# Weight sums in DRAM for every group of seven products, four groups more, and a new place for the sums of the second slot

## The chip, the cores and the metric

The kernel runs on one core of one Trainium2 chip. The metric is the device time of one execution in microseconds (us). Three runs of the kernel before gave a median of 2503.86 us, from 2502.97 to 2507.02.

The engines have short names in the profile: PE is the matrix engine (PEld its weight loads), DVE the vector engine, ACT the scalar engine, POOL the general-purpose engine and SP the engine that issues most DMAs. Each works through its own instructions in program order and waits on semaphores for the others.

## What is computed

256 tokens of width 2048 in fp32 go through two layers. Cut to what matters here:

```python
# layer 0: Mamba-2 mixer, then SwiGLU
h = h + mamba2_mixer(rmsnorm(h, a_norm_w), a_in_proj, ...)   # y = ssd(...) * silu(z); grouped rmsnorm; y @ out_proj
h = h + swiglu(rmsnorm(h, ffn_norm_w[0]), w_gate_up[0], w_down[0])
# shared keys, values and forget gates; layer 1: attention, then SwiGLU
k, v, cum = shared_kv(h, ...)
h = h + forgetting_attention(rmsnorm(h, b_norm_w), k, v, cum, w_q, q_norm_w, w_o)
h = h + swiglu(rmsnorm(h, ffn_norm_w[1]), w_gate_up[1], w_down[1])

def swiglu(h, w_gate_up, w_down):
    g, u = jnp.split(h @ w_gate_up, 2, axis=-1)
    return (jax.nn.silu(g) * u) @ w_down
```

`out_proj` is 4096 x 2048, `w_o` 2048 x 2048, `w_gate_up` 2048 x 11264 and `w_down` 5632 x 2048. Nearly all of the time is the products with these weights and with `in_proj`, `w_kvf` and `w_q`.

## The kernel before

**Weights.** All weights stream once from DRAM. The unit of a load is 512 KB, a tile `wraw` of 128 partitions by 1024 floats (two rows of 128 contracted values by 512 columns). There are six such buffers (`RAW`), and SP issues the next load when a buffer comes free. Each product is made in three matmuls of a shorter float type: ACT casts the unit to `whi` (`split_hi`, L271), DVE subtracts that from the unit to give `wlo` (`split_lo`, L277), and PE multiplies activation hi by weight hi, hi by lo and lo by hi (L563 to L565). A piece is one such split, used by six matmuls for a group, or twelve for an ordinary unit. Four pieces can be split ahead (`SPL`), so the cast of one piece waits until PE has finished the piece four before it. ACT, DVE and PE thus form a line with four places between its ends.

**Activations.** Each block of 512 activation channels lies transposed in a *slot* (tile `xT`, its hi and lo part). A projection's contracted width is cut into such slots, numbered kg.

**Groups of seven.** `pair` takes two neighbouring column blocks of an output. For most kg it makes their eight products in the plain way. For the kg in the tuple `crossed` it uses a scheme of Winograd's, seven products of six matmuls (L475, L476, L478) in place of eight. It needs sums of weights and sums of activations. The activation sums (tile `xS`) are made per slot in `sums_from` (four DVE operations, L624 to L627, then a cast by ACT and a subtraction by DVE), after an addition in `add_sums` (L641). `out_stage` makes those of some slots with the slot (`summed`) and others after the whole stage (`later`). The weight sums come in two ways:

- In the gate-and-up projections (`made=True`, pieces in the order f d c a e g b) a group loads five units. Two of them, c and a, are sums that were made in DRAM, and DVE makes two more additions (L429).
- In the out and down projections (`made=False`, order d g a c e b f) a group loads four units, and DVE makes four additions (L429).

The out projection of layer 0 (here *out0*) has groups at kg 4 and 6 of 8 (`WOUT`), the down projection of layer 0 (*dn0*) at 3 and 7, that of layer 1 (*dn1*) at 3, 6 and 9 of 11 and the attention's output projection (*wo*) at 2, each for two pairs of column blocks. The gate-and-up projections (*ffn0*, *ffn1*) have 20 groups each.

**Sums in DRAM.** `next_sum` takes one step: SP copies one weight unit to a DRAM tile `wsum` (L376), and POOL adds the partner of the sum begun before to it with an accumulating DMA (L378), once that copy has landed. The stream of loads calls it at every sixth load up to load 224 and at every twelfth after (`PACE`). Should a group's sum not be made when its load comes up, `load` calls `next_sum` until it is (L392). The load then follows on SP, where it waits until the accumulation has landed, and every later load stands behind it.

**Order.** The program is one stream of pieces. Everything else (normalisation, gates, the transposes into slots) is written as tasks in three queues (`urgent`, `mid`, `lazy`), which a planner works off between pieces. There is one exception: at piece d of a pair's first group `cross_step` (L452) empties the first two queues (`flow.finish_all(False)`, L463), whatever is in them, before it goes on.

**The gates before out0.** `z_done(g)` makes the gate of slot g of the eight that out0 contracts, and `gate_y` (L1064) finishes that slot: two products on DVE (L1069), two sums of squares on ACT (L1072), a root on DVE and POOL (L580, L582), two scalings on ACT (L1077), then transposes on PE (L595), cast by ACT (L273) and subtracted by DVE (L279). The slots 6 and 7 are finished while out0 is already running. After the last gate, `add_sums` is called for the slots in `WOUT`.

Of the kernel before, what the change touches and what calls it, by code (L numbers as in the profile page):

```python
# [230 lines left out]
def kernel(ctx: ExitStack, tc: tile.TileContext, xT_d, x_d, cols_d, rows_d, wdt_d, win_d,  # L231
# [191 lines left out]
    def split_cross(group, name):  # L423
# [7 lines left out]
        if group.cross.made:  # L431
            place, dead = {"e": "c", "b": "c"}, {"f": "f", "c": "d", "a": "a", "g": "g", "b": "c"}
            early, late = {}, {"c": ("c", "c", "d"), "e": ("c", "c", "g")}
        else:
# [6 lines left out]
        split_hi(hi, src)  # L441
        if name in early:
            add(*early[name])
        split_lo(hi, lo, src)
# [945 lines left out]
```

## Time and profile before

| | us |
|---|---|
| median of three runs | 2503.86 |
| lowest and highest of them | 2502.97, 2507.02 |
| the profiled execution | 2506.06 |
| its span in the trace | 2504.3 |
| PE busy in the span | 2482.6 |
| DVE busy | 1997.2 |
| ACT busy | 1425.8 |
| POOL busy | 105.4 |

The profiled execution is 2.2 us above the median. The span is what the profiler recorded; the other 1.8 us lie around it. A row of a time line reads: start, duration, engine, line of the kernel, operation, output and inputs; behind it, in brackets, how long the engine had been idle and what released it.

### The profile page before, as it was taken

The numbers are of one execution on the slowest core, as the hardware profiler recorded it, in microseconds if no ns is written. First come the engines' busy times: TensorE is split into PE (matmuls) and PEld (weight loads), VectorE is DVE, ScalarE is ACT, GpSimd is POOL, SyncE is SP. The second block draws the span as 40 slices with busy tenths as digits, with TensorE's granted clock in tenths as the row PEclk, the third lists the DMA queues.
The fourth block names the chain that finished last, engine by engine and source line by source line (L and its number), as shares of the span: only waits on it lengthen the run. The fifth ranks groups of instructions, "written<-read, shape, count | busy, mean of one in ns | idle before, by whom it ended". The sixth has DMA issues, their size and how long they took to land.

```text
span 2504.3 us, 31677 instructions
## 1 busy us (share of the span) xinstructions
PE 2482.6 (99%) x11434; PEld 2056.0 (82%) x11434; DVE 1997.2 (80%) x2569; ACT 1425.8 (57%) x1791; POOL 105.4 (4%) x132
## 2 busy tenths in 40 slices
PE   9999999999999999999999999999999999999999
PEld 7888888887878888888888888888878888888887
DVE  6677777778688999997767657678789898988867
ACT  6665566555456656564445556565565656555544
POOL 0000000000000000000000011010000000000000
PEclk9999999999999999999999999999999999999999
DMA  9887868677777888788676777665668776765564
GB/s 302 274 250 232 254 209 259 217 231 248 236 247 239 273 264 268 253 271 253 211 245 209 238 216 232 190 193 179 231 218 273 257 257 214 241 203 194 206 232 142
DMA packets 160205, 586.13 MB, mean 234 GB/s; under 512 B 17808, under 2 KB 18464, under 8 KB 158512
## 3 DMA queue, kind: packets, MB, share of 16 engines
q1 hardware_dynamic: 147024, 531.59, 61.8%
q0 software_dynamic: 13024, 52.52, 11.1%
q8 instruction: 90, 1.47, 0.2%
q14 instruction: 67, 0.55, 0.1%
HBM read 581.85 MB, written 86.07 MB: 267 GB/s over the span
## 4 chain that ended last, share of the span: by engine, by line
PE 93%; DVE 3%; DMA 2%; ACT 1%; issue 1%; SPq 0%; ACTq 0%; DVEq 0%
PE acc L564 23%; PE acc L563 23%; PE acc L565 23%; PE mis L476 4%; PE mis L478 4%; PE mis L475 4%; PE acc L475 3%; PE acc L476 3%; PE acc L478 3%; DVE wlo L277 2%; PE mis L595 1%; PE mis L1032 1%; DVE wraw L429 1%; DMA wraw<-in_wout_dram 1%; ACT whi L271 1%
## 5 line engine op out<-in xcount | busy, mean ns | idle before, releaser
L271 ACT CAST whi<-wraw 128x1024 fp32r<-128x1024 f32 (+1 forms) x956 | 982.9, 1049 | 699.6 <-PE acc L565 466.0
L277 DVE TENSOR_TENSOR wlo<-wraw,whi 128x1024 fp32r<-128x1024 f32 (+1 forms) x953 | 1140.4, 1220 | 299.8 <-ACT whi L271 291.3
L563 PE MATMUL acc<-whi,xT 128*128 128x512 f32 x2528 | 994.9, 394 | 5.4 <-ACT whi L271 4.1
L564 PE MATMUL acc<-wlo,xT 128*128 128x512 f32 x2528 | 986.2, 390 | 3.1 <-DVE wlo L277 3.1
L565 PE MATMUL acc<-whi,xT 128*128 128x512 f32 x2528 | 986.0, 390 | 0.0
L563 PEld LDWEIGHTS acc<-whi,xT 128*128 128x128 f32 x2528 | 475.4, 188 | 104.8 <-ACT whi L271 5.7
L564 PEld LDWEIGHTS acc<-wlo,xT 128*128 128x128 f32 x2528 | 475.7, 188 | 102.1 <-DVE wlo L277 5.8
L565 PEld LDWEIGHTS acc<-whi,xT 128*128 128x128 f32 x2528 | 475.3, 188 | 99.8
L279 DVE SCALAR_TENSOR_TENSOR wlo<-wraw,cols,whi 128x512 fp32r<-128x512 f32 x192 | 134.7, 747 | 72.1 <-ACT whi L273 71.7
L429 DVE TENSOR_TENSOR wraw<-wraw,wraw 128x1024 f32<-128x1024 f32 x144 | 176.4, 1225 | 6.2 <-DMA wraw<-in_wout_dram 1.4
L273 ACT ACTIVATE whi<-wraw,cols 128x512 fp32r<-128x512 f32 x192 | 127.6, 717 | 72.1 <-PE acc L565 55.1
L476 PE MATMUL mis<-wlo,xS 128*128 128x512 f32 x336 | 131.4, 391 | 2.8 <-DVE wlo L277 2.8
L475 PE MATMUL mis<-whi,xS 128*128 128x512 f32 x336 | 130.9, 390 | 0.7 <-DVE xT L277 0.7
L478 PE MATMUL mis<-whi,xS 128*128 128x512 f32 x336 | 130.7, 389 | 0.0
L378 POOL DMA_DIRECT2D wsum<-in_gu_dram x80 | 66.5, 831 | 1406.2 <-DMA wsum<-in_gu_dram 1379.1
L476 PE MATMUL acc<-wlo,xT 128*128 128x512 f32 x216 | 84.4, 391 | 2.1 <-DVE wlo L277 2.1
L475 PE MATMUL acc<-whi,xT 128*128 128x512 f32 x216 | 84.1, 389 | 0.0
L478 PE MATMUL acc<-whi,xT 128*128 128x512 f32 x216 | 84.1, 389 | 0.0
L476 PEld LDWEIGHTS mis<-wlo,xS 128*128 128x128 f32 x336 | 63.1, 188 | 18.1 <-DVE wlo L277 5.1
L475 PEld LDWEIGHTS mis<-whi,xS 128*128 128x128 f32 x336 | 63.0, 188 | 14.2 <-DVE xT L277 1.1
L478 PEld LDWEIGHTS mis<-whi,xS 128*128 128x128 f32 x336 | 63.1, 188 | 12.9
L271 ACT CAST xT<-mis 128x512 fp32r<-128x512 f32 x52 | 27.9, 589 | 52.4 <-PE mis L595 52.4
(241 smaller groups left out, 2050.3 us busy)
## 6 DMA issues: line engine op xcount, KB each, us to landing
wraw<-in_gu_dram SPq DMA_DIRECT2D x312, 512.0 KB, 5.6
wraw<-in_dn_dram SPq DMA_DIRECT2D x176, 512.0 KB, 5.5
wraw<-in_win_dram SPq DMA_DIRECT2D x159, 512.0 KB, 6.1
wsum<-in_gu_dram SPq DMA_DIRECT2D x80, 512.0 KB, 6.6
wsum<-in_gu_dram POOLq DMA_DIRECT2D x80, 512.0 KB, 8.3
wraw<-wsum SPq DMA_DIRECT2D x80, 512.0 KB, 4.7
wraw<-in_wout_dram SPq DMA_DIRECT2D x64, 512.0 KB, 6.4
wraw<-in_wq_dram SPq DMA_DIRECT2D x32, 512.0 KB, 4.5
```

What stands on the lines that cost most here:

```text
L271: nc.scalar.copy(out=hi, in_=src)
L273: nc.scalar.activation(hi, src, AF.Copy, scale=scal)
L277: nc.vector.tensor_tensor(out=lo, in0=src, in1=hi.bitcast(F32), op=ALU.subtract)
L279: nc.vector.scalar_tensor_tensor(out=lo, in0=src, scalar=scal, in1=hi.bitcast(F32), op0=ALU.mult, op1=ALU.subtract)
L378: nc.gpsimd.dma_start(out=old.tile, in_=old.other, accum_op=ALU.add)
L429: nc.vector.tensor_tensor(out=us[out].raw, in0=us[in0].raw, in1=us[in1].raw, op=ALU.add)
L475: nc.tensor.matmul(ps, lhsT=xh, rhs=hi[:, p, :], start=group.first and p == 0 and name not in own, stop=False)
L476: nc.tensor.matmul(ps, lhsT=xh, rhs=lo[:, p, :], start=False, stop=False)
L478: nc.tensor.matmul(ps, lhsT=xl, rhs=hi[:, p, :], start=False, stop=stop and p == 1)
L563: nc.tensor.matmul(b.ps[t], lhsT=xh, rhs=hi[:, j, :], start=u is b.units[0] and ks[j] == 0, stop=False)
L564: nc.tensor.matmul(b.ps[t], lhsT=xh, rhs=lo[:, j, :], start=False, stop=False)
L565: nc.tensor.matmul(b.ps[t], lhsT=xl, rhs=hi[:, j, :], start=False, stop=last and j == len(ks) - 1)
```

## The change

All groups now take the form that only the gate-and-up projections had: five loads, two sums from DRAM, two additions on DVE. Out0 gets groups at kg 2, 4 and 6, and dn1 at 3, 5, 7 and 9, which is one more for each of the two pairs of column blocks, four more in all. There are now 120 sums in DRAM, where there were 80. None is begun in the first 24 loads; from there to load 224 there is one for each six loads, and after that one for each ten. The activation sums of slot 1 of the two gate-and-up projections are made when that slot is made, not after the stage. The sums for out0's slots 2 and 4 are asked for at gate 6, those of slot 6 at gate 7 as before. `add_sums` works in another buffer.

```diff
-WOUT, DN0, DN1 = (4, 6), (3, 7), (3, 6, 9)
+WOUT, DN0, DN1 = (2, 4, 6), (3, 7), (3, 5, 7, 9)
-PACE = (224, 6, 12)
+PACE = (24, 224, 6, 10)
@@ class Cross
-        self.order = "fdcaegb" if made else "dgacebf"
+    ORDER = "fdcaegb"
@@ def pair
+        adjacent = len(crossed) > 1 and crossed[-1] == crossed[-2] + 1
             if kg in crossed:
-                if not (made and kg > crossed[0]):
+                if not (adjacent and kg == crossed[-1]):
                     order += rights
                     rights = []
                 (b11, b21), (b12, b22) = us
-                if made:
-                    c, a = Sum(b22.src, b12.src), Sum(b22.src, b21.src)
-                    sums.extend((c, a))
-                    first = {"f": b12, "d": b21, "c": Unit(None, kg, c, NB, [1, 3]),
-                             "a": Unit(None, kg, a, NB, [1, 3]), "g": b11}
-                else:
-                    first = {"d": b21, "g": b11, "+": b22, "f": b12}
+                c, a = Sum(b22.src, b12.src), Sum(b22.src, b21.src)
+                sums.extend((c, a))
+                first = {"f": b12, "d": b21, "c": Unit(None, kg, c, NB, [1, 3]),
+                         "a": Unit(None, kg, a, NB, [1, 3]), "g": b11}
@@ def split_cross
-            place, dead = {"a": "d", "c": "+", "e": "d", "b": "+"}, {"c": "g", "e": "d", "b": "+", "f": "f"}
-            early = {"g": ("+", "f", "+"), "c": ("d", "f", "d")}
-            late = {"d": ("d", "d", "+"), "c": ("+", "g", "d")}
+        place, dead = {"e": "c", "b": "c"}, {"f": "f", "c": "d", "a": "a", "g": "g", "b": "c"}
+        late = {"c": ("c", "c", "d"), "e": ("c", "c", "g")}
@@ def stream
-                pace = PACE[1] if i < PACE[0] else PACE[2]
-                if i % pace == pace - 1:
+                pace = PACE[2] if i < PACE[1] else PACE[3]
+                if i >= PACE[0] and i % pace == pace - 1:
                     next_sum()
@@ def out_stage
-                for kg in later:
-                    add_sums(nxt[kg])
@@ def ffn_up, took
-                if xs[1].adder is not None:
-                    flow.finish(xs[1].adder)
@@ def z_done
-            if g == G - 1:
+            if g >= G - 2:
                 for kg in WOUT:
-                    add_sums(ys[kg])
+                    if (kg < G - 2) == (g == G - 2):
+                        add_sums(ys[kg])
@@
-    xs2, r2 = out_stage(ys, wout_d, C_F0, WOUT, summed=(2,), later=(1,))
+    xs2, r2 = out_stage(ys, wout_d, C_F0, WOUT, summed=(1, 2))
-    xs4, r4 = out_stage(oT, wo_d, C_F1, (2,), summed=(2,), later=(1,))
+    xs4, r4 = out_stage(oT, wo_d, C_F1, (2,), summed=(1, 2))
```

PE has 10760 instructions in place of 10784, which is 24 matmuls of 512 columns fewer. SP has 60 rows more (20 loads and 40 copies), POOL 40 more (accumulations), and DVE 24 additions fewer. The line numbers of the changed kernel are some 4 to 9 lower than those of the kernel before. Its instructions stand in another order at three places.

**Out0's first pair of column blocks, PE.** In the kernel before, the transposes of slot 7 (inputs `xs`, outputs `mis`) stand between pieces of ordinary units (outputs `acc`), as those of slot 6 do some way ahead of them:

```order
L565 MATMUL acc_4718<-whi_4682,xT_3301 128x512
L563 MATMUL acc_4719<-whi_4682,xT_3301 128x512
L564 MATMUL acc_4719<-wlo_4683,xT_3301 128x512
L565 MATMUL acc_4719<-whi_4682,xT_3301 128x512
L595 MATMUL mis_4778<-ident,xs_2541 128x128 x4
L595 MATMUL mis_4787<-ident,xs_2541 128x128 x4
L563 MATMUL acc_4718<-whi_4712,xT_3301 128x512
L564 MATMUL acc_4718<-wlo_4713,xT_3301 128x512
L565 MATMUL acc_4718<-whi_4712,xT_3301 128x512
```

In the changed kernel the group at kg 2 stands here. After its piece f (the six products with `xS`) come the transposes of slot 6 and then those of slot 7, and piece d only behind both:

```order
L466 MATMUL acc_4601<-whi_4615,xS_4406 128x512
L467 MATMUL acc_4601<-wlo_4616,xS_4406 128x512
L469 MATMUL acc_4601<-whi_4615,xS_4406 128x512
L466 MATMUL acc_4601<-whi_4615,xS_4406 128x512
L467 MATMUL acc_4601<-wlo_4616,xS_4406 128x512
L469 MATMUL acc_4601<-whi_4615,xS_4406 128x512
L586 MATMUL mis_4698<-ident,xs_2529 128x128 x4
L586 MATMUL mis_4707<-ident,xs_2529 128x128 x4
L586 MATMUL mis_4728<-ident,xs_2529 128x128 x4
L586 MATMUL mis_4737<-ident,xs_2529 128x128 x4
L466 MATMUL mis_4746<-whi_4633,xT_3521 128x512
L467 MATMUL mis_4746<-wlo_4634,xT_3521 128x512
```

The queues that piece d empties now hold the ends of two gates, and no product stands between the transposes of the two.

**The same place, ACT.** Before, casts of weights (`whi<-wraw`) stand between the steps of slot 7's gate, from slot 6's transposes in the first row to slot 7's own in the last two:

```order
L273 ACTIVATE xT_4641<-mis_4651,cols 128x256 x2
L1072 ACTIVATE zs_4563,ssg_4660<-xs_2541 128x512
L271 CAST whi_4664<-wraw_4488 128x1024
L271 CAST whi_4682<-wraw_4531 128x1024
L1072 ACTIVATE zs_4565,ssg_4660<-xs_2541 128x512
L271 CAST whi_4712<-wraw_4549 128x1024
L1077 ACTIVATE xs_2541<-xs_2541,rs_4703 128x512 x2
L271 CAST xS_4597<-xsum_4707 128x4x128
L271 CAST whi_4736<-wraw_4581 128x1024
L271 CAST whi_4759<-wraw_4609 128x1024
L273 ACTIVATE xT_4777<-mis_4778,cols 128x256 x2
L273 ACTIVATE xT_4777<-mis_4787,cols 128x256 x2
```

Now, the last cast ahead of the gates' ends is that of piece e, and the next one comes behind both:

```order
L272 CAST whi_4690<-wraw_4509 128x1024
L1069 ACTIVATE xs_2529<-xs_2529,rs_4652 128x512 x2
L274 ACTIVATE xT_4697<-mis_4698,cols 128x256 x2
L274 ACTIVATE xT_4697<-mis_4707,cols 128x256 x2
L1064 ACTIVATE zs_4597,ssg_4716<-xs_2529 128x512
L1064 ACTIVATE zs_4599,ssg_4716<-xs_2529 128x512
L1069 ACTIVATE xs_2529<-xs_2529,rs_4723 128x512 x2
L274 ACTIVATE xT_4727<-mis_4728,cols 128x256 x2
L274 ACTIVATE xT_4727<-mis_4737,cols 128x256 x2
L272 CAST xS_4654<-ysum_4753 128x4x128
L272 CAST whi_4761<-wraw_4552 128x1024
```

The steps of slot 7's gate (its squares and its scaling) moved in between the transposes of slots 6 and 7.

**The start of ffn0, DVE.** Before, the sums of slot 1 (L641, and 624 to 627 with the `xS` subtraction) stand among the splits and additions of the first group:

```order
L277 TENSOR_TENSOR wlo_6145<-wraw_5980,whi_6144 128x1024
L277 TENSOR_TENSOR wlo_6155<-wraw_5956,whi_6154 128x1024
L429 TENSOR_TENSOR wraw_5956<-wraw_5956,wraw_6000 128x1024
L277 TENSOR_TENSOR wlo_6167<-wraw_6000,whi_6166 128x1024
L277 TENSOR_TENSOR wlo_6178<-wraw_5956,whi_6177 128x1024
L624 TENSOR_TENSOR xsum_6195<-y_6123 128x128
L625 TENSOR_TENSOR xsum_6195<-y_6123 128x128
L626 TENSOR_TENSOR xsum_6195<-y_6123,xsum_6195 128x128
L627 TENSOR_TENSOR xsum_6195<-y_6123,xsum_6195 128x128
L277 TENSOR_TENSOR wlo_6201<-wraw_6035,whi_6200 128x1024
L277 TENSOR_TENSOR xS_6194<-xsum_6195,xS_6194 128x4x128
L641 TENSOR_TENSOR y_6215<-xT_5282 128x512
```

Now only splits and additions stand there (L278 is `split_lo`, L428 the addition):

```order
L278 TENSOR_TENSOR wlo_6166<-wraw_6001,whi_6165 128x1024
L428 TENSOR_TENSOR wraw_6001<-wraw_6001,wraw_5966 128x1024
L278 TENSOR_TENSOR wlo_6185<-wraw_6025,whi_6184 128x1024
L278 TENSOR_TENSOR wlo_6195<-wraw_6001,whi_6194 128x1024
L428 TENSOR_TENSOR wraw_6001<-wraw_6001,wraw_6045 128x1024
L278 TENSOR_TENSOR wlo_6207<-wraw_6045,whi_6206 128x1024
L278 TENSOR_TENSOR wlo_6218<-wraw_6001,whi_6217 128x1024
L278 TENSOR_TENSOR wlo_6238<-wraw_6080,whi_6237 128x1024
```

The sums of slot 1 have moved some 80 rows up, into the second pair of out0.

**A late group of ffn1, SP.** Before, the group's two sums are loaded from tiles `wsum` that were copied some hundreds of loads earlier:

```order
L398 DMA wraw_17485<-in_gu_dram 128x1024
L398 DMA wraw_17487<-wsum_12494 128x1024
L398 DMA wraw_17489<-wsum_12858 128x1024
L398 DMA wraw_17502<-in_gu_dram 128x1024
L398 DMA wraw_17515<-in_gu_dram 128x1024
```

Now the copies (L375) stand right among the group's loads, that of the second sum (`wsum_18267`) with one load between it and its own:

```order
L397 DMA wraw_18264<-in_gu_dram 128x1024
L375 DMA wsum_18267<-in_gu_dram 128x1024
L397 DMA wraw_18266<-wsum_18095 128x1024
L375 DMA wsum_18272<-in_gu_dram 128x1024
L397 DMA wraw_18271<-wsum_18267 128x1024
L397 DMA wraw_18287<-in_gu_dram 128x1024
```

From the 81st sum on the copies have caught up with the loads: 13 of the last 40 sums have six or fewer loads between their copy and their own load. Ten of them are in ffn1, with distances of 4, 5, 6, 2, 3, 6, 1, 1, 6 and 1 in their order, and three in dn1, with 1 each. In the kernel before the smallest such distance is 97 loads.

## Rows read from the trace of the kernel before

**Rows 1.** The page, first part: busy us, share of the span, instructions

```profile
span 2504.3 us, 31677 instructions
PE 2482.6 (99%) x11434; PEld 2056.0 (82%) x11434; DVE 1997.2 (80%) x2569; ACT 1425.8 (57%) x1791; POOL 105.4 (4%) x132
```

**Rows 2.** Time line of PE, first and last of 60 matmuls without a pause

```profile
690.72 0.39 PE L563 MATMUL acc<-whi,xT 128*128 128x512 f32 x1
...
704.09 0.39 PE L565 MATMUL acc<-whi,xT 128*128 128x512 f32 x1
```

**Rows 3.** Busy time by stretches: stretch, length, each engine, PEclk, DMA share, GB/s

```profile
560.00:620.00 60.00, 56.23 (x248) 44.69 (x247) 52.38 (x57) 30.31 (x34) 2.52 (x4) 1.00 0.76 233
...
725.00:750.00 25.00, 22.31 (x88) 16.98 (x87) 23.04 (x33) 13.51 (x16) 1.91 (x2) 0.93 0.68 204
...
1205.00:1212.00 7.00, 6.61 (x30) 5.12 (x29) 6.91 (x7) 4.62 (x6) 0.00 (x0) 1.00 0.32 90
1740.00:1760.00 20.00, 18.21 (x85) 14.54 (x84) 18.79 (x26) 10.96 (x18) 0.82 (x1) 1.00 0.95 315
1825.00:1866.00 41.00, 37.16 (x162) 28.96 (x161) 36.62 (x45) 23.43 (x26) 0.81 (x1) 1.00 0.74 231
```

**Rows 4.** Time line at the start of ffn0, PE and ACT

```profile
738.74 0.62 ACT L271 CAST xS<-xsum 128x512 fp32r<-128x512 f32 x1 [2.77 <-DVE xsum L627]
...
740.36 0.50 PE L563 MATMUL acc<-whi,xT 128*128 128x512 f32 x1 [1.05 <-ACT whi L271]
741.62 0.50 PE L564 MATMUL acc<-wlo,xT 128*128 128x512 f32 x1 [0.76 <-DVE wlo L277]
...
742.97 0.63 PE L563 MATMUL acc<-whi,xT 128*128 128x512 f32 x1
```

**Rows 5.** Stretches around a pause at the start of ffn0 and of ffn1

```profile
732.00:746.00 14.00, 11.31 (x40) 7.93 (x39) 12.87 (x20) 7.74 (x10) 0.00 (x0) 0.88 0.71 228
1829.00:1845.00 16.00, 13.26 (x55) 9.72 (x54) 14.87 (x23) 8.57 (x10) 0.00 (x0) 1.00 0.72 240
```

**Rows 6.** Time line in out0: slot 6's transposes, then gate 7's steps

```profile
540.10 1.03 PE L595 MATMUL mis<-ident,xs 128*128 128x128 f32 x8
...
543.90 0.63 ACT L1072 ACTIVATE zs<-xs 128x512 f32<-128x512 f32 x1 [1.60 <-DVE xs L1069]
...
548.12 1.08 POOL L582 TENSOR_TENSOR rs<-ms,mhalf 128x2 f32<-128x2 f32 x1 [12.10 <-DVE ms L580]
...
549.23 1.34 ACT L1077 ACTIVATE xs<-xs,rs 128x512 f32<-128x512 f32 x2 [1.16 <-POOL rs L582]
```

**Rows 7.** The page, DMA issues: count, KB each, median us to landing

```profile
wsum<-in_gu_dram SPq DMA_DIRECT2D x80, 512.0 KB, 6.6
wsum<-in_gu_dram POOLq DMA_DIRECT2D x80, 512.0 KB, 8.3
wraw<-wsum SPq DMA_DIRECT2D x80, 512.0 KB, 4.7
```

**Rows 8.** DMA issues from 1225 to 1250 us, few loads in flight

```profile
wsum<-in_gu_dram SPq DMA_DIRECT2D x1, 512.0 KB, 5.2
wsum<-in_gu_dram POOLq DMA_DIRECT2D x1, 512.0 KB, 5.7
```

**Rows 9.** DMA issues from 1953 to 1962 us, many loads in flight

```profile
wsum<-in_gu_dram SPq DMA_DIRECT2D x1, 512.0 KB, 6.7
wsum<-in_gu_dram POOLq DMA_DIRECT2D x1, 512.0 KB, 9.8
```

**Rows 10.** Time line in ffn1, a second group: load of d, splits of a

```profile
1905.55 0.33 SPq L398 DMA_DIRECT2D wraw<-in_gu_dram  x1
...
1917.65 1.05 ACT L271 CAST whi<-wraw 128x1024 fp32r<-128x1024 f32 x1 [1.67 <-PE acc L565]
...
1918.74 1.23 DVE L277 TENSOR_TENSOR wlo<-wraw,whi 128x1024 fp32r<-128x1024 f32 x1 [0.23 <-ACT whi L271]
...
1921.76 0.39 PE L476 MATMUL mis<-wlo,xS 128*128 128x512 f32 x1
```

**Rows 11.** Time line in ffn1, a first group: load of d, split of a

```profile
1886.96 0.33 SPq L398 DMA_DIRECT2D wraw<-in_gu_dram  x1
...
1903.20 1.06 ACT L271 CAST whi<-wraw 128x1024 fp32r<-128x1024 f32 x1
```

More of the change, by code (lines that the diff above doesn't have):

```diff
@@ L207, with __init__ @@
 class Cross:
-    def __init__(self, left, right, parts, made):
-        self.left, self.right, self.parts, self.made, self.ps = left, right, parts, made, {}
-        self.order = "fdcaegb" if made else "dgacebf"
+    ORDER = "fdcaegb"
+    def __init__(self, left, right, parts):
+        self.left, self.right, self.parts, self.ps = left, right, parts, {}
 class Group:
@@ L334, in narrow, with pair @@
         blocks.append(b)
-    def pair(xs, sources, done, fills, crossed, parts, made=False):
+    def pair(xs, sources, done, fills, crossed, parts):
         both = [Block(xs, d, f) for d, f in zip(done, fills)]
-        x = Cross(*both, parts, made)
+        x = Cross(*both, parts)
         order, rights = [], []
+        adjacent = len(crossed) > 1 and crossed[-1] == crossed[-2] + 1
         for kg in range(len(xs)):
@@ L361, in pair @@
                 rights += us[1]
-        if made and len(crossed) > 1:
+        if adjacent:
             n = next(i for i in range(len(order) - 1, 0, -1) if isinstance(order[i], Group))
@@ L429, in add @@
             nc.vector.tensor_tensor(out=us[out].raw, in0=us[in0].raw, in1=us[in1].raw, op=ALU.add)
[L431 to L434, printed above, removed]
-            place, dead = {"a": "d", "c": "+", "e": "d", "b": "+"}, {"c": "g", "e": "d", "b": "+", "f": "f"}
-            early = {"g": ("+", "f", "+"), "c": ("d", "f", "d")}
-            late = {"d": ("d", "d", "+"), "c": ("+", "g", "d")}
+        place, dead = {"e": "c", "b": "c"}, {"f": "f", "c": "d", "a": "a", "g": "g", "b": "c"}
+        late = {"c": ("c", "c", "d"), "e": ("c", "c", "g")}
         src = us[place.get(name, name)].raw
@@ L440, in split_cross @@
         lo = wspl.tile([P, 2, NB], F32R, tag="wlo", name=nm("wlo"))
[L441 to L444, printed above, removed]
+        split(hi, lo, src)
         ready = flow.work("V", 1.22, flow.work("A", 1.05, flow.at["E"]) + LAT)
@@ L495, in stream @@
                 if isinstance(u, Group):
-                    pieces += [(u, n) for n in u.cross.order]
+                    pieces += [(u, n) for n in Cross.ORDER]
                     units += u.units.values()
@@ L617, in sums_of, with sums_from @@
         yield from sums_from(dst, half, y)
-    def sums_from(dst, half, y):
+    def sums_from(dst, half, y, s=None):
         if half == 0:
             dst.sums = slot([P, 4, 2, 2, P], F32R, "xS")
-        s = tok("xsum").rearrange("p (n t) -> p n t", t=P)
+        s = (tok("xsum") if s is None else s).rearrange("p (n t) -> p n t", t=P)
         sub = ALU.subtract
@@ L630, in sums_from, with add_sums @@
         yield A(0.6) + V(0.6)
-    def add_sums(dst):
+    def add_sums(dst, apart=True):
         def run():
@@ L638, in run @@
             for half in range(2):
-                y = tok("y").rearrange("p (f t) -> p f t", t=T)
+                if apart:
+                    y, x = (lambda c: (c[:, 0], c[:, 1]))(phase.tile([P, 2, NB], F32, tag="c4", name=nm("ysum")))
+                else:
+                    y, x = tok("y"), None
+                y = y.rearrange("p (f t) -> p f t", t=T)
                 part = [s[:, i, 2 * half:2 * half + 2, :].bitcast(F32) for i in range(2)]
@@ L642, in run @@
                 yield V(0.66)
-                yield from sums_from(dst, half, y)
+                yield from sums_from(dst, half, y, x)
         dst.adder = spawn(run(), flow.lazy)
@@ L696, in parts_to_h, with out_stage @@
         return run
-    def out_stage(xs, w_d, wcol, crossed, summed=(), later=()):
+    def out_stage(xs, w_d, wcol, crossed, summed=()):
         ss = const.tile([P, NT, 4], F32, name=nm("ss"))
@@ L777, in took @@
                 x[0] = y
-                if xs[1].adder is not None:
-                    flow.finish(xs[1].adder)
                 return parts(y)
             pair(xs, gu_d[2 * nb:2 * nb + 2], (lambda ps, x=x: gate(x[0], ps), lambda ps, x=x, nb=nb: up(x[0], ps, nb)),
-                 (None, acts[nb]), (1, 2) if 0 < nb < NFB - 1 else (2,), took, made=True)
+                 (None, acts[nb]), (1, 2) if 0 < nb < NFB - 1 else (2,), took)
         return acts
```

2 lines of the change are left out of this document (1 added, 1 removed).

## Prediction

> **What bounds the kernel now.** I read the page's first part first: PE is busy for 2482.6 of 2504.3 us [rows 1]. So the time is the number of matmuls times their spacing, plus the places where PE waits. The spacing comes from an undisturbed stretch of PE's time line: 60 matmuls of 512 columns start within 13.37 us, or 0.2267 us each [rows 2]. A piece of six takes 1.36 us, a group of seven pieces 9.5. Second, I went through the span in stretches to see where PE is not busy [rows 3]: 3.77 us in out0's first pair (560 to 620), 2.69 at the start of ffn0 (725 to 750), 0.39 in dn0 (1205 to 1212; dn1 has one like it), 1.79 in wo (1740 to 1760), 3.84 at the start of ffn1 (1825 to 1866). Each pause costs some 0.16 us more than shows as idle, since a matmul's row lasts 0.39 us while the next could start after 0.2267 [rows 2]; for some 20 pauses that is 3 us. Third, the clock: around ffn0's pause the granted clock was 0.88 of full speed, around ffn1's 1.00 [rows 5]. At ffn0 a matmul lasts 0.63 us [rows 4], and seven of them were 0.2 us further apart than at full speed, which is 1.4 us. All this together is about 17.4 us: 4.6 in out0 (3.77 and five pauses), 4.8 at ffn0 (with the clock), 4.9 at ffn1, 2.0 in wo, 0.55 each in dn0 and dn1. No more than that can be won by better supply.
>
> **The change part by part.**
>
> *Four more groups.* They save 24 matmuls x 0.2267 = 5.4 us. In-group supply gets easier too: an out or down group had 7 subtractions and 4 additions on DVE, 11 x 1.23 us (one subtraction's time [rows 10]) = 13.5 against PE's 9.5. Now it has 9 of them, 11.1. Both are still above 9.5, but buffers hold four pieces, and plain pieces between the groups let DVE catch up.
>
> *The old pauses.* At the start of ffn0 PE waits for a cast of ACT (1.05) and for a subtraction of DVE (0.76); ACT, ahead of that, waited 2.77 us for the sums of slot 1 on DVE [rows 4]. Those sums leave this place. They go to out0's second pair, where PE never pauses and DVE, by the stretch from 620 to 725 us, is busy for three quarters of the time, so they cost nothing there; without that cover they would cost their DVE time, some 5 us. Of the 12.8 us at ffn0, ffn1, wo, dn0 and dn1, I take 11.0 as gone, and leave 1.8 for one pair of such waits (1.05 and 0.76). The bounds are 6 and 12.8. In out0 the pauses of the first pair (4.6) came from the sums of slots 4 and 6, made between splits. Slot 4's are partly made earlier now, slot 6's not. I let the 4.6 go and put 2.0 back for slot 6 (bounds 0 and 4.6).
>
> *A new wait in out0.* The group at kg 2 starts when the gates of slots 6 and 7 are unfinished, and its piece d empties the queues first. The order on PE and ACT shows that nothing but the gates' ends stands there. PE is done with piece f; ACT then casts piece e, which had no free buffer before (1.05 [rows 10]), scales slot 6 (1.34) and hands over: 2.5 us. Then comes the chain that the trace of before shows once [rows 6]: transposes at 540.10; squares at 543.90, so 3.80 later; two squares of 0.63; the root (1.08 on POOL); scaling, which begins at 549.23, 1.11 after POOL's start, and takes 1.34 [rows 6]. That is 3.80 + 1.26 + 1.11 + 1.34 = 7.5, with hand-overs 8; less the transposes themselves, in which PE works (1.03), some 7.0. In the kernel before all this lies under plain pieces and costs nothing; now PE has nothing else. So PE stands still for 2.5 + 7.0 = 9.5 us. Piece g follows late, as its cast comes behind slot 7's casts and half of a sum: 1.0 more. Together 10.5, bounds 6 (should half the chain be over before PE gets there) and 14.
>
> *The clock after it.* One of two like pauses cost 1.4 us in clock, the other none [rows 5]. A pause of 9.5 us is longer than both, so I add 1.4. The Trainium skill (TensorE: Matmul & The Clock Gate, "HAM oscillation — how this bites in real kernels") says that a kernel whose matmuls wait for DMA in each round starts every round at the low clock. The trace agrees at ffn0 and not at ffn1 (0.88 and 1.00); by the page the two largest new waits below would pay 1.4 us each, by the trace about one of them.
>
> *Sums just in time.* From the 81st sum on SP copies sums shortly before they are used. Where the copy has one load between it and its own, the chain is: copy, POOL's accumulation, load. SP waits at that load. In the second group of a pair, the copy would be issued behind d's load, at 1905.95, and ACT casts a at 1917.65; DVE ends its subtraction at 1919.97, and PE wants it at 1921.76 [rows 10]. So there are 11.7 + 1.8 = 13.5 us. In a first group, there are 1903.20 - 1887.4 = 15.8 [rows 11], with the same margin 17.6. No such chain is in the trace, so I bound it. With few loads in flight copy and accumulation take 5.2 and 5.7 [rows 8]; with 0.5 for POOL's start and 4.7 for the load [rows 7] that is 16.1. With many loads it is 6.7, 9.8 [rows 9], 0.5 and 4.7: 21.7. By the medians [rows 7] it is 6.6 + 0.5 + 8.3 + 4.7 = 20.1. I take 17.3, nearer to the light row, because SP, held at the load, issues no loads that could compete. That makes 3.8 us each at the two second groups with distance 1 (the 94th and 98th sum), 0.9 where the copy stands one load earlier (90th; 16.4 us there), and nothing at the four first groups (one in ffn1, three in dn1): 8.5 us. At 16.1 it is 5.2. At 21.7 it is 2 x 8.2 + 5.3 + 4 x 4.1 + a little = 38. I add 1.4 for the clock behind one of the two.
>
> *None in the first 24 loads.* PE's last early pause ends before the first copy could matter: transfers land in the order of issue there, and the loads that PE waits for were issued ahead of that copy. No gain, no loss. *More transfers*: 40 sums and 20 loads more are 100 transfers of 512 KB on top of some 1080, on DMA engines that are busy for 0.68 to 0.76 of the stretches around the two layers' starts [rows 3]. Loads get a little slower; I take zero for it, with up to 5 us above and nothing below.
>
> **Sum**: -5.4 (matmuls) -11.0 (ffn, wo, dn) -4.6 +2.0 (out0's old waits) +10.5 (gates) +1.4 (clock) +8.5 (sums) +1.4 (clock) = +2.8 us on the profiled execution's 2506.06, so 2508.9. That execution lies 2.2 above the median; on the median the same sum gives 2503.86 + 2.8 = **2506.7**. A measurement of this kernel can tell about 0.2%, 5.0 us, from no change.
>
> **The rivals.**
>
> *The supply gain wins.* The sums come in time, since a held SP leaves the engines to them (16.1 us, which costs 5.2), and the gates' chain is half over when PE arrives (6). Then -5.4 - 11.0 - 2.6 + 6 + 1.4 + 5.2 = -6.4, and with all of the old waits gone (-12.8 and -4.6) -10.2: 2494 to 2497. For it: the light row was taken with five loads about [rows 8]. Against it: emptying the queues leaves PE no work to hide the chain.
>
> *The sums come late.* At the medians' 20.1 the second groups wait 6.6 each, the 90th sum 3.7, the four first groups 2.5 each: 27 us in place of 8.5, which gives 2503.86 + 2.8 + 18.5 = 2525; at 21.7 it is 2536. This decides from a chain of about 17.6 us on, where the first groups begin to wait as well. For it: the copy is issued right behind other loads, and beside an accumulation the row of many loads shows 9.8. The Trainium skill (DMA: Bandwidth & Descriptors, "Issuing engines are not separate DMA queues") speaks for it: what POOL issues shares the same engines with SP's loads. The two accumulations, 5.7 and 9.8 [rows 8, 9], agree.
>
> *DVE was not what held ffn's start.* If the splits themselves are short there, 11.0 shrinks to 6: 2511.7.
>
> *It does not do what it says.* The four groups are in PE's order, and the 24 matmuls are gone; I give this nothing.
>
> **How the numbers follow.** The forecast, with its terms near what I took, 0.45 (2500 to 2513); supply gain 0.22; late sums 0.23; ffn's start held otherwise 0.10. The likeliest case's own range crosses both bounds of 5 us. From the cases: faster by more than 0.2% (below 2498.9) 0.25, which is nearly all of the first rival and a little of the forecast; slower (above 2508.9) 0.37, the late sums, most of the last and the forecast's upper fifth; within 0.2% the rest, 0.38. The range for 8 in 10 leaves out the far ends of the two rivals: 2495 to 2525.
>
> **What would show it.** In out0's first pair PE should have one pause of some 9 us, in two or three pieces around the transposes, with ACT's scaling and POOL's root in it; if it is below 6, that step was too dear. At the starts of ffn0 and ffn1 the waits for `whi` and `wlo` should be down to 2 us in all. In late ffn1 there should be waits of PE for ACT, and of ACT for `wraw<-wsum`, of about 4 us at two second groups, none at most others; waits at dn1's three would mean that the chain is over 17.6 us. A median under 2495 or over 2525 would say that one of the two large terms, gates or sums, was off by more than its half.

## The result, and the profile after

The changed kernel takes 2550.46 us (median of four runs, 2547.09 to 2552.08), the kernel before 2504.53 (four runs; the 2503.86 of the table before is the median of three of them). The ratio is 1.0181, with an interval from 1.0163 to 1.0198. It is 46 us slower, where 3 us were forecast. The profiled executions lie closer together than the medians: 2547.09 and 2506.06, with spans 41.0 us apart.

The page's first lines of the changed kernel; they answer to [rows 1]:

```profile
span 2545.3 us, 31879 instructions
PE 2497.1 (98%) x11410; PEld 2064.3 (81%) x11410; DVE 1990.1 (78%) x2577; ACT 1443.6 (57%) x1815; POOL 137.0 (5%) x172
```

The 24 matmuls are gone (11434 to 11410), and yet PE is busy 14.5 us longer. Most of that is slower matmuls (a matmul's row ahead of a pause also counts as busy for its full length), and the stretches of the changed kernel show where they are. Columns are as in [rows 3]: stretch, length, busy time and count for PE, PEld, DVE, ACT and POOL, then the granted clock, the DMA share and GB/s.

```profile
535.00:545.00 10.00, 7.07 (x20) 5.61 (x21) 2.87 (x4) 3.87 (x6) 0.00 (x0) 0.66 0.39 136
...
545.00:575.00 30.00, 21.13 (x91) 16.72 (x90) 21.24 (x34) 16.94 (x28) 2.36 (x3) 0.83 0.33 89
...
725.00:752.00 27.00, 26.39 (x120) 21.41 (x119) 23.04 (x30) 18.60 (x29) 2.35 (x3) 1.00 0.67 196
1740.00:1770.00 30.00, 28.96 (x135) 23.78 (x134) 27.38 (x38) 18.50 (x28) 0.81 (x1) 1.00 0.79 254
1825.00:1886.00 61.00, 60.21 (x268) 49.15 (x267) 52.28 (x54) 38.17 (x45) 3.18 (x4) 1.00 0.77 246
2080.00:2100.00 20.00, 16.38 (x64) 12.83 (x63) 12.67 (x13) 8.69 (x11) 0.81 (x1) 0.91 0.92 252
2115.00:2150.00 35.00, 28.68 (x118) 22.29 (x118) 23.61 (x22) 16.82 (x19) 1.63 (x2) 0.90 0.91 278
2170.00:2200.00 30.00, 24.69 (x95) 18.97 (x94) 19.89 (x17) 15.12 (x16) 2.46 (x3) 0.89 0.93 283
2345.00:2412.00 67.00, 57.18 (x213) 44.74 (x212) 43.27 (x46) 28.54 (x30) 4.07 (x5) 0.86 0.88 264
```

The starts of ffn0 (725), of ffn1 (1825) and wo (1740) have most or part of their time back: there is 0.61, 0.79 and 1.04 us of idle time where [rows 3] have 2.69, 3.84 and 1.79. Two places have got worse. One is out0's first pair, from 535 to 575; the other is late ffn1 and dn1, from 2080 on. In all the stretches shown of these two the clock is below 1.00.

To put numbers on it I took the starts of all matmuls of both traces and summed what lies between neighbours above the spacing of 0.2267 us: gaps over 0.48 us as pauses, those from 0.3 to 0.48 as low clock.

| place | before: pauses, low clock | after: pauses, low clock | difference |
|---|---|---|---|
| out0 | 4.6, 1.2 | 15.6, 3.5 | +13.3 |
| start of ffn0 | 3.4, 2.0 | 0.8, 0.4 | -4.2 |
| dn0 | 0.5, 0.1 | 0, 0 | -0.6 |
| wo | 2.1, 0.3 | 1.2, 0.3 | -0.9 |
| start of ffn1 | 4.9, 0.8 | 1.1, 0.5 | -4.1 |
| late ffn1 (from 2060) | 0, 0.5 | 18.4, 6.0 | +23.9 |
| dn1 | 0.5, 0.1 | 12.9, 7.2 | +19.5 |

With 24 x 0.2267 = 5.4 us for the matmuls and 2 us less in the kernel's first 50 us this gives +39.5; the spans differ by 41.0. Of the 2 us, the pause at 40 us is taken up at e7; the pauses of the first 13 us differ between executions of the same instructions (2.2 us of them in e2, 4.0 in e5).

**Late ffn1 and dn1.** One late sum, the 98th, in the changed kernel's time line (columns as in [rows 4]; L375 is the copy, L377 the accumulation, L397 a load):

```profile
2172.77 0.50 SPq L375 DMA_DIRECT2D wsum<-in_gu_dram  x1
...
2179.34 0.81 POOL L377 DMA_DIRECT2D wsum<-in_gu_dram  x1 [17.12 <-DMA wsum<-in_gu_dram]
...
2187.66 0.33 SPq L397 DMA_DIRECT2D wraw<-wsum  x1
...
2191.53 2.94 ACT L272 CAST whi<-wraw 128x1024 fp32r<-128x1024 f32 x3 [8.39 <-DMA wraw<-wsum]
...
2192.63 0.80 PE L466 MATMUL mis<-whi,xS 128*128 128x512 f32 x1 [4.34 <-ACT whi L272]
2193.89 0.80 PE L467 MATMUL mis<-wlo,xS 128*128 128x512 f32 x1 [0.46 <-DVE wlo L278]
2194.48 0.63 PE L469 MATMUL mis<-whi,xS 128*128 128x512 f32 x1
```

Each step is released by the one above. The copy is issued at 2172.77 and POOL starts 6.6 us later, on its landing. SP can issue the load only at 2187.66, 8.3 us after POOL began, when the accumulation has landed. ACT has the sum at 2191.53, 18.8 us after the copy was issued. PE waits for ACT (4.34) and again for DVE (0.46), and its matmuls then run at the low clock (0.63 us each, as in [rows 4]). The six sums that stop PE, three in ffn1 (90th, 94th, 98th) and three in dn1 (108th, 110th, 112th), have chains of 18.0 to 20.3 us (landings of the load against issue of the copy). In them the copy took 5.9 to 7.5 us, the accumulation 5.7 to 8.3, the load 3.8 to 5.4. The 96th, in a first group of ffn1, had a chain of 17.4 us, and PE did not wait for ACT there. The waits of SP, in the summary of waits (released by, us in total, times, longest):

```profile
SPq L397 <- DMA wsum<-in_gu_dram: 61.8, 7, 11.5
SPq L397 <- DMA wsum<-in_dn_dram: 35.5, 3, 13.0
```

SP stood ten times in front of a sum that was not made, for up to 13.0 us, with all later loads behind it.

**Out0.** PE's waits in the changed kernel from 525 to 575 us, behind the ACT row that ended the first of them:

```profile
537.20 1.26 ACT L1046 ACTIVATE zs<-acc,rstd 128x512 f32<-128x512 f32 x2
...
537.93 0.80 PE L554 MATMUL acc<-whi,xT 128*128 128x512 f32 x1 [5.06 <-ACT zs L1046]
555.50 0.33 PE L586 MATMUL mis<-ident,xs 128*128 128x128 f32 x1 [2.56 <-ACT xs L1069]
556.11 1.05 PE L586 MATMUL mis<-ident,xs 128*128 128x128 f32 x7 [0.29 <-ACT xs L1069]
563.05 2.37 PE L586 MATMUL mis<-ident,xs 128*128 128x128 f32 x8 [5.89 <-ACT xs L1069]
```

The last three are the gates that were forecast: waits for the scaling of slot 6 and of slot 7 ahead of their transposes. The first was not forecast. An ordinary matmul waits for ACT's `zs` (L1046), which reads the `acc` banks of the last gate projection.

### The profile page after: what moved, and what is told of

Read it like the earlier page. It is cut to its first block, busy times and chain, and to the rows that moved or that the text cites. A ratio compares the mean times of both kernels' runs of the same rounds, so it can differ in the third digit from the quotient of the medians.

```text
span 2545.3 us, 31879 instructions
## 1 busy us (share of the span) xinstructions
PE 2497.1 (98%) x11410; PEld 2064.3 (81%) x11410; DVE 1990.1 (78%) x2577; ACT 1443.6 (57%) x1815; POOL 137.0 (5%) x172
## 4 chain that ended last, share of the span: by engine, by line
PE 68%; DMA 6%; DVE 3%; ACT 1%; issue 1%; SPq 0%; POOL 0%; ACTq 0%; POOLq 0%; DVEq 0%
PE acc L554 16%; PE acc L556 16%; PE acc L555 16%; PE mis L467 4%; PE mis L469 4%; PE mis L466 3%; DMA wsum<-in_gu_dram 3%; PE acc L467 3%; PE acc L469 3%; PE acc L466 3%; DMA wraw<-wsum 2%; DVE wlo L278 2%; PE mis L586 1%; DMA wsum<-in_dn_dram 1%; ACT whi L272 1%
## 5 line engine op out<-in xcount | busy, mean ns | idle before, releaser
L278 DVE TENSOR_TENSOR wlo<-wraw,whi 128x1024 fp32r<-128x1024 f32 (+1 forms) x965 | 1155.2, 1221 | 344.6 <-ACT whi L272 337.4
L272 ACT CAST whi<-wraw 128x1024 fp32r<-128x1024 f32 (+1 forms) x968 | 994.8, 1050 | 713.9 <-PE acc L556 436.1
L554 PE MATMUL acc<-whi,xT 128*128 128x512 f32 x2464 | 970.6, 394 | 5.5 <-ACT zs L1046 5.1
L555 PE MATMUL acc<-wlo,xT 128*128 128x512 f32 x2464 | 961.3, 390 | 0.8 <-DVE wlo L278 0.8
L556 PE MATMUL acc<-whi,xT 128*128 128x512 f32 x2464 | 961.6, 390 | 0.0
L554 PEld LDWEIGHTS acc<-whi,xT 128*128 128x128 f32 x2464 | 463.9, 188 | 102.0 <-ACT zs L1046 5.3
L556 PEld LDWEIGHTS acc<-whi,xT 128*128 128x128 f32 x2464 | 463.5, 188 | 97.8
L555 PEld LDWEIGHTS acc<-wlo,xT 128*128 128x128 f32 x2464 | 464.0, 188 | 95.8 <-DVE wlo L278 1.8
L466 PE MATMUL mis<-whi,xS 128*128 128x512 f32 x360 | 146.0, 406 | 20.1 <-ACT whi L272 20.1
L467 PE MATMUL mis<-wlo,xS 128*128 128x512 f32 x360 | 146.4, 407 | 3.9 <-DVE wlo L278 3.9
L428 DVE TENSOR_TENSOR wraw<-wraw,wraw 128x1024 f32<-128x1024 f32 x120 | 147.0, 1225 | 4.1
L469 PE MATMUL mis<-whi,xS 128*128 128x512 f32 x360 | 145.3, 404 | 0.0
L377 POOL DMA_DIRECT2D wsum<-in_gu_dram x80 | 66.2, 828 | 1105.4 <-DMA wsum<-in_gu_dram 1105.4
L466 PEld LDWEIGHTS mis<-whi,xS 128*128 128x128 f32 x360 | 70.5, 196 | 37.5 <-ACT whi L272 22.7
L467 PE MATMUL acc<-wlo,xT 128*128 128x512 f32 x232 | 91.6, 395 | 2.5 <-DVE wlo L278 2.4
L466 PE MATMUL acc<-whi,xT 128*128 128x512 f32 x232 | 91.1, 393 | 0.0
L469 PE MATMUL acc<-whi,xT 128*128 128x512 f32 x232 | 90.6, 390 | 0.0
L469 PEld LDWEIGHTS mis<-whi,xS 128*128 128x128 f32 x360 | 70.7, 196 | 14.7
```

The costliest lines, as they stand in the source:

```text
L272: nc.scalar.copy(out=hi, in_=src)
L278: nc.vector.tensor_tensor(out=lo, in0=src, in1=hi.bitcast(F32), op=ALU.subtract)
L377: nc.gpsimd.dma_start(out=old.tile, in_=old.other, accum_op=ALU.add)
L428: nc.vector.tensor_tensor(out=us[out].raw, in0=us[in0].raw, in1=us[in1].raw, op=ALU.add)
L466: nc.tensor.matmul(ps, lhsT=xh, rhs=hi[:, p, :], start=group.first and p == 0 and name not in own, stop=False)
L467: nc.tensor.matmul(ps, lhsT=xh, rhs=lo[:, p, :], start=False, stop=False)
```

## The experiments

The theory after the result has three parts: late sums cost 43 us; the group at kg 2 of out0 costs 13; the sums of slot 1, made with the slot, give 9 back.

**e1: a sum for each 7 loads.** The smallest distance between a copy and its sum's load is then 64 loads, with the same groups and the same transfers.

```diff
-PACE = (24, 224, 6, 10)
+PACE = (24, 224, 6, 7)
```

> The changed kernel with one number altered: past load 224 a sum in DRAM for each 7 loads, not 10, so that at least 64 loads lie between a sum's copy and its own load. Theory (late sums): the waits of PE behind sums made just in time in late ffn1 and dn1, with the low clock behind them, cost 43 us of the changed kernel's 2550; they vanish, and the time is 2504 to 2511. Rival (traffic): the 100 transfers more slow the loads wherever they stand; then PE still waits in ffn1 or dn1 and the time stays over 2530.

Measured: 2505.5 us (2503.54 to 2507.58), 1.0001 times the kernel before (0.9991 to 1.001). So 45 us go with one number, and the 100 transfers more cost nothing that can be seen when they come early. The stretches of e1 (columns as above), out0 and then what was late ffn1 and dn1's first groups:

```profile
525.00:575.00 50.00, 36.11 (x148) 28.68 (x147) 32.10 (x52) 26.40 (x44) 4.28 (x5) 0.83 0.47 136
...
2040.00:2170.00 130.00, 130.00 (x588) 107.89 (x587) 117.99 (x117) 78.44 (x84) 6.54 (x8) 1.00 0.91 296
2310.00:2380.00 70.00, 68.94 (x302) 56.06 (x301) 61.51 (x73) 40.23 (x42) 0.00 (x0) 1.00 0.69 229
```

PE has no idle time at all in late ffn1, at a DMA share of 0.91, which is that of the stretches with pauses in the changed kernel. A DMA share of 0.9 is thus no sign of trouble by itself. Out0 is as bad as in the changed kernel.

**e4: a sum for each 9 loads**, the dose between. Three sums have one load between copy and own load.

```diff
-PACE = (24, 224, 6, 10)
+PACE = (24, 224, 6, 9)
```

> The changed kernel with a sum for each 9 loads past load 224. Three sums (the 102nd in ffn1, the 118th and 120th in dn1) then have one load between copy and own load, where the changed kernel has six such; the others have six or more. Theory (late sums): three pauses of 4 to 6 us with 2 us of low clock each, 17 to 24 us over e1, and nothing elsewhere. Rival (traffic): a time near the changed kernel's 2550, with waits spread over ffn1 and dn1.

Measured: 2526.14 us in a single run, 20.6 over e1's median. SP's waits and PE's at two of the three places:

```profile
SPq L397 <- DMA wsum<-in_dn_dram: 25.6, 3, 12.8
```

```profile
2221.66 0.79 PE L466 MATMUL mis<-whi,xS 128*128 128x512 f32 x1 [5.25 <-ACT whi L272]
2222.92 0.79 PE L467 MATMUL mis<-wlo,xS 128*128 128x512 f32 x1 [0.47 <-DVE wlo L278]
...
2477.30 0.79 PE L466 MATMUL mis<-whi,xS 128*128 128x512 f32 x1 [3.14 <-ACT whi L272]
2478.56 0.79 PE L467 MATMUL mis<-wlo,xS 128*128 128x512 f32 x1 [0.47 <-DVE wlo L278]
```

The pauses stand where the distances said. Where the third would stand, at 2502, there is only a wait of 0.70 for DVE and no low clock: there the distance of one load was enough, with a chain of 16.4 us where the other two have 19.8 and 18.6. The sum of pauses and low clock above e1's is 9 in ffn1 and 9 in dn1. So the theory's place was right and the count was two and a small one, not three. With one run the time itself says little; the places and sizes of the waits carry it.

**e2: out0's groups at kg 4 and 6.** In addition to e1:

```diff
-WOUT, DN0, DN1 = (2, 4, 6), (3, 7), (3, 5, 7, 9)
+WOUT, DN0, DN1 = (4, 6), (3, 7), (3, 5, 7, 9)
```

> As e1 and with out0's groups at kg 4 and 6 alone, as in the kernel before (12 matmuls more than e1). Theory (group at kg 2 too early): out0's three new waits, 5 us for a bank of PSUM and 10 us around two gates, with 3 us of low clock, come from the group at kg 2 alone; they go, less 2.7 us for the matmuls, and the time is 2493 to 2498. Rival (gates late): the sums of slots 2 and 4, asked for at gate 6, hold up the gates themselves; then a wait for a gate of 5 us or more is left in out0 and the time is over 2500.

Measured: 2491.82 us (2490.83 to 2492.78), 0.9946 of the kernel before (0.9932 to 0.9959); 13.7 less than e1 with 12 matmuls more. It is faster than both kernels. Its out0:

```profile
525.00:570.00 45.00, 45.00 (x212) 37.52 (x212) 33.17 (x52) 28.87 (x47) 4.87 (x6) 1.00 0.77 229
560.00:620.00 60.00, 59.34 (x271) 48.56 (x270) 51.44 (x63) 34.35 (x46) 3.23 (x4) 1.00 0.87 280
```

The second row is the stretch of [rows 3] in which 3.77 us were idle; now it is 0.66. The gates' ends lie under plain pieces, and the sums of slot 4, asked for a gate earlier, do not hold the gates up. With no group at kg 2 there are no sums of slot 2 here, so for slot 4 the rival falls and for slot 2 this run is no test; e5, which asks for the sums of two slots at gate 6 as the changed kernel does, bears on that.

**e5: the first group at kg 3**, in place of kg 2, beside e1's other settings.

```diff
-WOUT, DN0, DN1 = (2, 4, 6), (3, 7), (3, 5, 7, 9)
+WOUT, DN0, DN1 = (3, 4, 6), (3, 7), (3, 5, 7, 9)
```

> As e1, with out0's groups at kg 3, 4 and 6: as many matmuls as e1 and the changed kernel, but 16 pieces of ordinary work more than they have ahead of the first group. Theory (group at kg 2 too early): the right-hand column block begins one kg later, 5.4 us, so the 5 us wait for its bank goes; slot 6's gate ends under the added pieces, and of the two gate waits (2.9 and 6.2 us) at most one is left; 2493 to 2499. Rival (three groups are too many for DVE): what is won at the gates comes back as waits for wlo in the three groups, 5 us or more, and the time is over 2501.

Measured: 2499.5 us (2496.91 to 2502.52), 0.9973 of the kernel before (0.9964 to 0.9982), just above what the theory allowed. PE's waits in out0:

```profile
540.30 0.50 PE L554 MATMUL acc<-whi,xT 128*128 128x512 f32 x1 [0.56 <-ACT zs L1046]
562.43 0.38 PE L586 MATMUL mis<-ident,xs 128*128 128x128 f32 x1 [3.25 <-ACT xs L1069]
563.05 1.76 PE L586 MATMUL mis<-ident,xs 128*128 128x128 f32 x7 [0.24 <-ACT xs L1069]
571.89 0.50 PE L467 MATMUL acc<-wlo,xT 128*128 128x512 f32 x1 [0.76 <-DVE wlo L278]
578.55 0.51 PE L466 MATMUL mis<-whi,xS 128*128 128x512 f32 x1 [1.16 <-ACT whi L272]
579.81 0.80 PE L467 MATMUL mis<-wlo,xS 128*128 128x512 f32 x1 [0.76 <-DVE wlo L278]
```

(The added work, one kg of two blocks, is 48 matmuls or 10.9 us; "16 pieces" was a slip.) The wait for the bank falls from 5.06 to 0.56, as the right-hand block starts one kg later; of the two gates one is left (3.25). That is the theory. But between the groups at 3 and 4 the rival shows as well, at about half its price: 2.7 us of waits for ACT and DVE. Three groups did not get through here without a pause.

**e6: a third group at kg 5.**

```diff
-WOUT, DN0, DN1 = (4, 6), (3, 7), (3, 5, 7, 9)
+WOUT, DN0, DN1 = (4, 5, 6), (3, 7), (3, 5, 7, 9)
```

> As e2, with a third out0 group at kg 5, so that the count of matmuls is that of e1. Theory: both gates are over when the first group starts at kg 4, no wait comes in their place, and 12 matmuls go: 2.7 us under e2, 2487 to 2490. Rival (DVE): with three groups close together DVE needs 11.1 us for each 9.5 us of PE, 4.8 us in all, and the four pieces of lead (5.4 us) are spent: waits for wlo of 2 to 5 us, 2490 to 2495.

Measured: 2508.22 us (2506.9 to 2511.19), 16 over e2 and outside both expectations. Its larger waits:

```profile
582.05 0.50 PE L466 MATMUL mis<-whi,xS 128*128 128x512 f32 x1 [0.87 <-ACT whi L272]
583.31 0.50 PE L467 MATMUL mis<-wlo,xS 128*128 128x512 f32 x1 [0.76 <-DVE wlo L278]
...
617.88 0.77 PE L554 MATMUL acc<-whi,xT 128*128 128x512 f32 x1 [5.29 <-DVE h L674]
...
710.83 0.77 PE L554 MATMUL acc<-whi,xT 128*128 128x512 f32 x1 [5.28 <-DVE h L674]
```

The rival's waits are there (some 3 us at 580 to 586). Most of it is something else: 5.3 us at the end of each pair, where PE waits for DVE to read banks into `h`. I had overlooked that groups at 5 and 6 are neighbours: `pair` then moves the last group behind the left block's other units (`adjacent`, `both[0].after`), so the left block ends late, and the next block, which needs its banks, finds them not yet read. That is read from the code and the two waits; no run takes it apart. So e6 says little of DVE as a limit, and it shows again what a bank costs that is asked for too early.

**e3: the kernel before, with the sums of slot 1 made with the slot.**

```diff
-    xs2, r2 = out_stage(ys, wout_d, C_F0, WOUT, summed=(2,), later=(1,))
+    xs2, r2 = out_stage(ys, wout_d, C_F0, WOUT, summed=(1, 2))
-    xs4, r4 = out_stage(oT, wo_d, C_F1, (2,), summed=(2,), later=(1,))
+    xs4, r4 = out_stage(oT, wo_d, C_F1, (2,), summed=(1, 2))
```

> The kernel before with one thing changed: the sums of slot 1 of both gate-and-up projections are made with the slot. Theory: this alone takes the waits at the starts of ffn0 and ffn1 away, 9 us, so 2493 to 2498. Rival (waits move): DVE is late there for other reasons, or the sums wait elsewhere; 2501 to 2505.

Measured: 2497.22 us (2496.34 to 2499.36), 0.9968 of the kernel before (0.9957 to 0.998), 8.5 us less. Its stretches at the starts of ffn0 and ffn1, which answer to [rows 3]:

```profile
725.00:752.00 27.00, 26.37 (x117) 21.47 (x116) 24.05 (x29) 16.42 (x21) 1.54 (x2) 1.00 0.76 244
...
1825.00:1866.00 41.00, 40.43 (x183) 33.22 (x182) 35.39 (x37) 25.17 (x27) 0.81 (x1) 1.00 0.78 263
```

Idle time falls from 2.69 to 0.63 and from 3.84 to 0.57, and the clock is 1.00 in both. What the changed kernel won at the starts of ffn0 and ffn1 comes with this edit alone.

**e7: sums from the first load on**, beside e2's settings.

```diff
-PACE = (24, 224, 6, 7)
+PACE = (0, 224, 6, 7)
```

> As e2, but with sums in DRAM from the first load on. Theory (transfers land in order and PE's early pauses wait for earlier loads): no difference, 2490.8 to 2492.8. Rival (a copy among the first loads delays one that PE waits for): a pause of 1 to 2 us more before 13 us, 2493 to 2494.

Measured: 2491.46 us (2490.07 to 2495.06), 0.994 of the kernel before (0.9926 to 0.9953), as e2: by the medians, leaving the first 24 loads without sums does nothing. The traces show a little more. PE's largest wait in e7 from 30 to 50 us, and that stretch in e7 and in e2:

```profile
39.86 0.83 PE L822 MATMUL mis<-ones,red 128*128 128x2 f32 x6 [1.70 <-DVE red L816]
```

```profile
30.00:50.00 20.00, 18.30 (x83) 15.11 (x82) 15.05 (x10) 10.37 (x13) 2.39 (x3) 0.91 0.90 287
30.00:50.00 20.00, 20.00 (x97) 16.76 (x97) 16.14 (x15) 9.85 (x13) 0.71 (x1) 1.00 0.54 175
```

The three kernels with sums among the first loads all have this wait (0.56 us in the kernel before, 1.11 in e3, 1.70 in e7), and the seven without have no idle time of PE in these 20 us. So the rival was right that a pause goes with the early copies, though not before 13 us, and it is smaller than the spread of e7's runs (5.0 us). Why DVE is late there was not followed.

**e8: dn1's groups at kg 3, 6 and 9**, beside e2's settings.

```diff
-WOUT, DN0, DN1 = (4, 6), (3, 7), (3, 5, 7, 9)
+WOUT, DN0, DN1 = (4, 6), (3, 7), (3, 6, 9)
```

> As e2, with dn1's groups at kg 3, 6 and 9 as in the kernel before, so 12 matmuls more and no group more than before anywhere. Theory (matmuls are all that the two groups bring): 2.7 us over e2, 2494 to 2495. Rival (the groups in every second kg keep DVE late in dn1): half of that, 2492.5 to 2493.5.

Measured: 2494.23 us (2491.51 to 2495.14), 0.9948 of the kernel before (0.9936 to 0.9961). Beside e7, from the same set of runs, it is 2.8 us longer, beside e2 2.4; its runs spread over 3.6 us, so it leans to the matmuls (2.7) without settling it against half of that. It has as many matmuls as e3 and is 3.0 us under it by medians of two sets of runs, whose kernel before differs by 0.45 and whose intervals just overlap. That is what the new form of the out and down groups gives, together with the early sums for out0, the other pace and the first 24 loads; no run separates these.

## Why the prediction was wrong

**The matmuls**: right, 24 fewer. **The old pauses** of ffn0, ffn1, wo and dn0: right in cause for ffn0 and ffn1 (e3) and nearly in size, 9.8 us in the table where 11.0 was taken with dn1's. In dn1 a new wait of DVE came with the closer groups (e1 has 1.4 us of pauses there, the kernel before 0.5). **Nothing from the first 24 loads**: right within what the medians can tell (e7), but the reason given, that PE's last early pause ends before the first copy could matter, was not: there is one at 40 us, of 0.56 us in the kernel before, that is gone without the early copies.

**The gates in out0**: the mechanism was right and so was the size. PE's three waits there are 2.56, 0.29 and 5.89 us, 8.7 as idle time, and 10.2 from start to start with the two short gaps behind the transposes; 10.5 was taken. The 2.0 us put back for slot 6 were too much (0.3).

**A step was missing in out0.** The group at kg 2 makes `pair` put the right-hand blocks of kg 0 and 1 ahead of it. So the second column block is due 48 matmuls, 10.9 us, after the first, and needs its two `acc` banks, which ACT had not yet emptied of the last gate projection. I had compared what stands between the transposes in PE's order, and not from where on the block's banks are new. That is 5.06 us (e5: 0.56), and 13.3 in all for out0 where the sum had +9.3.

**Sums just in time: the step that failed.** The forecast had 8.5 and 1.4 us of clock, the runs show 43 to 45 (e1). The table's 43.4 are 16.3 of waits at ffn1's three second groups (8.5 was taken), 12.4 more of waits in dn1 (nothing was taken), 2.1 of smaller waits for DVE in ffn1, and 12.6 of low clock (1.4 was taken). The forecast named the sums and the places in ffn1 correctly, and the times it read there hold: with the measured chains, its 13.5 and 16.4 us give waits of 3.9 to 5.6 us, within 0.8 of what PE shows, and none at the 96th sum. Three terms failed.

- *The chain.* 17.3 was taken, 18.0 to 20.3 measured (mean 19.1), which is between the two rows that the prediction called many loads (21.7) and few (16.1), and near the medians of the profile's page (20.1). The reason given for the low value, that a held SP issues no loads that could compete, does not hold: the next sum's copy was already under way, and its accumulation followed from POOL. While SP waits for the 98th sum, the DMA view of the changed kernel from 2175 to 2190 us (40 slices; busy share in tenths, then GB/s) reads

```profile
DMA  7589899578797866886999997318589986969897
GB/s 295 229 295 393 350 371 240 164 262 262 251 317 306 350 251 229 175 120 120 197 197 131 142 240 153 66 22 120 76 120 175 208 109 109 197 131 208 197 328 273
```

  In the second half two accumulations follow each other, the next sum's beside this one's. The engines are busy in most of these slices and yet move less than 250 GB/s in all but two. From 2183.8 to 2187.6 us only the accumulations' queue moves anything (packets, MB, share of the 16 engines):

```profile
q0 software_dynamic: 128, 0.46, 77.8%
```

  So accumulations alone kept the engines busy for 0.78 of that time. That their bytes are few may in part be the view's count: with 40 accumulations more, this queue's bytes on the page rise from 52.5 to 73.5 MB, which is each one's 512 KB once. The Trainium skill (DMA: Bandwidth & Descriptors, "Issuing engines are not separate DMA queues") was the better guide here: transfers of POOL and of SP share the engines. The trace agrees, with POOL's 0.78 of the same 16 engines.
- *The margin in dn1.* The time from copy to use in a first group was read in ffn1 (17.6 us) and applied to dn1, whose trace of before has no such group. In dn1 it is less. The 108th sum:

```profile
2333.19 0.50 SPq L375 DMA_DIRECT2D wsum<-in_dn_dram  x1
...
2346.34 0.33 SPq L397 DMA_DIRECT2D wraw<-wsum  x1
```

```profile
2349.44 0.39 PE L469 MATMUL mis<-whi,xS 128*128 128x512 f32 x1
2352.40 0.80 PE L466 MATMUL mis<-whi,xS 128*128 128x512 f32 x1 [2.57 <-ACT whi L272]
2353.66 0.80 PE L467 MATMUL mis<-wlo,xS 128*128 128x512 f32 x1 [0.46 <-DVE wlo L278]
```

  PE was ready for the subtraction's result at 2349.9 (two spacings after 2349.44) and got it at 2353.66, 3.8 us late, with a chain of 18.0. So the margin was 14.2 (by the same reckoning 15.2 at the 110th and 15.5 at the 112th), and all three sums of dn1 stopped PE; the forecast had them at nothing. Why the time there is shorter than in ffn1 was not followed.
- *The clock.* 1.4 us was taken for one pause in two. All six pauses for late sums, and those of out0, were followed by slow matmuls: some 1.8 us each in ffn1 (6.0 less 0.5, by three) and 2.2 in dn1 (7.2 less e1's 0.6, by three), 12 us in all. Behind the wait for the 108th sum the granted clock was at the lower of its two levels, 0.50 of 2.4 GHz:

```profile
2352.40:2359.00 6.60, 6.14 (x14) 4.48 (x15) 6.51 (x7) 4.55 (x6) 0.00 (x0) 0.50 0.79 305
```

  Here the Trainium skill (TensorE: Matmul & The Clock Gate, "HAM oscillation — how this bites in real kernels") is borne out: behind each of the six waits for a transfer PE started again at the low clock. The one pause before that did not [rows 5] was made of shorter waits with matmuls between, as the one that did; why these two differ stays open.

So the rival "the sums come late" was what happened, at its own price of 2525 too low by the last two points. Neither it nor the forecast took the clock behind each late sum, nor the time in dn1 from dn1.

What the change would be without its two faults is e2: 0.9946 of the kernel before, some 13.9 us. By the runs, e3's edit gives 8.5 of it, the new form with what goes along with it some 3.0 (e8 against e3), and dn1's two added groups 2.4 to 2.8.

## What to carry to other kernels

A copy, an accumulation and a load in a row are one latency: where a stock of such sums is worked off, count how many loads lie between each copy and its use to the very end, since a rate that looks ample on average runs out there, and the in-order queue that waits then holds everything behind it. Price a new wait with the waits of the other engines behind it and with the clock that follows, and take the time that is available from the place itself, not from a like one. When work moves ahead, look for what it occupies (banks, buffers) as closely as for what it waits for.

## What the runs showed of the hardware

512 KB accumulations in DRAM took 5.7 to 8.3 us in the six late chains. Where their queue alone was at work (2183.8 to 2187.6 us), it held a share of 0.78 of the engines with 0.46 MB, 121 GB/s as the view counts them; e1's stretch of 130 us moved 296 GB/s at 0.91. After PE's long waits, 2.6 to 5.9 us as idle time shows them, its matmuls of 512 columns ran 0.43 us apart in place of 0.2267 for a while; the granted clock was 0.50 in the 6.6 us behind one of them (2352.40 to 2359.00) and 0.66 over the ten microseconds around another (the stretch from 535 to 545 above).
